# Gated linear attention and retention with their outputs transposed: channels on the partitions, head norm by a product with a 0/1 matrix

## The chip, the cores and the metric

The kernel runs on one core of one Trainium2 chip. A core has five engines with queues of their own: TensorE (PE, matrix products; its weight loads have a row of their own, PEld), VectorE (DVE), ScalarE (ACT), GpSimd (POOL) and SyncE (SP, which here only starts DMA transfers). The metric is the device time of one execution in microseconds (us). The kernel before took 1004.41 us as the median of three runs (1003.13 to 1007.25).

## What is computed

Two layers run over a sequence of 1024 tokens with 1024 features. Each layer normalises and modulates its input, projects it, runs three groups of heads side by side, and projects their concatenation back:

```python
h = rms_norm(x, pre_gain) * (1.0 + scale) + shift
proj = h @ w_in
(aq, ak, av, ag, rq, rk, rv, rg, gq, gk, gv, gg, ga) = jnp.split(proj, IN_SPLITS, axis=-1)
a_out = sliding_window_attention(aq, ak, av, sinks) * jax.nn.silu(ag)
r = retention(rq, rk, rv)                       # 4 heads of 64
r_out = rms_norm(r).reshape(B, S, RET_W) * jax.nn.silu(rg)
log_a = jax.nn.log_sigmoid(ga @ gla_gate_w + gla_gate_b) / 16
g = gated_linear_attention(gq, gk, gv, log_a)   # 4 heads, keys 32 wide, values 64 wide
g_out = rms_norm(g, gla_norm_gain).reshape(B, S, GLA_W) * jax.nn.silu(gg)
y = jnp.concatenate([a_out, r_out, g_out], axis=-1) @ w_out
x = x + gate * rms_norm(y, post_gain)
```

What matters here is the end of the two recurrent groups. Retention and gated linear attention (GLA) each give, per token, four heads of 64 values; every head is divided by the root of its mean square over its 64 values, and the result is multiplied by SiLU of a gate of the same 256 channels.

## The kernel before

The sequence is cut into eight tiles of 128 tokens, and tiles into four pairs. The normalised input of a pair lies transposed in SBUF (`hT`, features on the partitions). A value that needs more than one TensorE pass of precision is split in two parts of type float32r, hi and lo (`split`), and a projection adds three products, hi·hi, lo·hi and hi·lo, over eight slices of 128 features: 24 matrix products (`accum`). Products of plain float32 operands appear in the trace as two records each.

The order of TensorE's instructions is the order in which the program is written out. The program keeps a clock of its own (`clk`), which each product moves on by an assumed cost. Side work stands in jobs (generators), which yield the time that must pass, or the flag that must be set, before their next step. `accum` calls `pump` after every seventh product, and `pump` runs each job that is due. So the latencies in the table `L` (`hn1`, `gz1` and so on) decide between which products of a projection a job's instructions stand; TensorE then waits at run time if the operands are not there. The other engines take their instructions in an order that the framework sets, and SP's queue issues nearly all transfers.

A layer goes through these stages. (1) Gates: for each pair the projections `gg` (GLA's gate, with 16 more columns `ga` for the decay logits: 272 columns) and `rg` (retention's gate), one tile of 128 tokens at a time, tokens on the partitions (`do_gates`, `project`). SiLU of the gate is stored to DRAM (`sgS`, `srS`). `gla_logits` transposes the 16 logit columns and, for every four tiles, `gla_log` turns them into log decays with exp and ln. (2) Retention: per pair the projections `rq`, `rk`, `rv`; a job `ret_core` per tile transposes q and k, forms the scores `sc`, the output `po` and the state `stR`. (3) GLA: projections `gqk` and `gv`, with a job `gla_core` per pair; it uses decays from `gla_decays`, writes masked scores `scz`, the output `po` and the state `stG`. (4) Attention projections, attention, its gate `ag`; (5) the output projection, which reads the concatenated heads from DRAM (`mixS`, and in the second layer `mixF`), with features on the partitions.

Around the change: the output of a tile, `po`, is a PSUM tile with 128 tokens on the partitions and 4 x 64 values on the free axis. In retention (lines 1170 to 1176) the state part is two float32 products of 128 columns, and each head adds one product that holds the head's 128x128 scores as weights and moves 64 columns of values. In GLA (lines 1117 to 1122) the state part is one product of 256 columns, and the heads add the same. PSUM has eight banks, three for projections (`mm`) and five for everything else (`aux`).

`head_norm_gate` (line 960) then squares `po` on ACT (L963), adds up each head on DVE (L965), scales and adds eps (L632), raises to the power -0.5 on POOL (L633), multiplies on DVE (L968), multiplies by the gate loaded from DRAM (L969), waits for `hn1`, transposes the two halves on TensorE (L176), and `store_mix` (L944) splits the transposed tile in hi (ACT) and lo (DVE) and stores both.

The ScalarE keeps one set of function tables at a time; a change of set is an instruction of its own in the trace (ACT_TABLE_LOAD). `gla_log` loads a set with exp and ln each time it runs.

Of the kernel before, what the change touches and what calls it, by code (L numbers as in the profile page):

```python
# [56 lines left out]
def host_constants():  # L57
    f = np.float32
    c = {}
    c["ident"] = np.eye(P, dtype=f)  # L60
    i = np.arange(P)
    rope = np.power(f(10000.0), -np.arange(0, 64, 2, dtype=f) / f(64))
    ret = f(1.0) / np.power(f(10000.0), np.arange(32, dtype=f) / f(31))
    freq = np.concatenate([rope, ret]).astype(f)
    c["freq"] = np.broadcast_to(freq, (P, 64)).copy()
    c["causal"] = (i[:, None] <= i[None, :]).astype(f)
    c["mask2"] = ((i[:, None] <= i[None, :]) & (i[:, None] // 32 == i[None, :] // 32)).astype(np.int32)
    c["curmask"] = (i[:, None] >= i[None, :]).astype(np.int32)
# [12 lines left out]
    c["hmask"] = (i[:, None] // 32 == np.arange(4)[None, :]).astype(f)  # L81
    return c
# [7 lines left out]
def trunk(ctx: ExitStack, tc: tile.TileContext, ins, cst, out):  # L90
# [157 lines left out]
    V.memset(mhalf, -0.5)  # L248

# [4 lines left out]
    sgS = dr.tile([NT, P, 256], F32, name="sgS")  # L254
    srS = dr.tile([NT, P, 256], F32, name="srS")
# [248 lines left out]
    def load(l, name, first=None):  # L504
# [12 lines left out]
        def conv(kc, st):  # L517
# [106 lines left out]
    def project_T(pm, l, hf, w, c):  # L624
# [3 lines left out]
              lambda b, k: both(h0[:, b, k, :], h1[:, b, k, :]))  # L628

# [135 lines left out]
    hmask = cload("hmask")  # L765
    qdec = cload("qdec")
# [177 lines left out]
    def store_mix(l, t, kt0, src, n):  # L944

        if l == DEPTH - 1 and t >= PLAIN:
            mf = t1()
            mfv = mf[:, 0:n * P].rearrange("p (k q) -> p k q", k=n)
            copy("mf", mfv, src)
            dma("smh", mixF[t, :, kt0:kt0 + n, :], mfv)  # L950
# [9 lines left out]
    def head_norm_gate(l, t, po, gate, scale, eps, kt0):  # L960

        sq = t1()
        A.activation(sq, po, AF.Square)  # L963
        ss = small(4)
        V.tensor_reduce(ss, h4(sq), AX.X, ALU.add)  # L965
# [18 lines left out]
    def gla_logits(l, t, pg, pa):  # L984
        ga = small(16)
        A.activation(ga, pa, AF.Copy)
        dma("ssg", sgS[t], silu(pg))
# [10 lines left out]
    def gla_log(l, i):  # L998
# [5 lines left out]
        e, la = t2(), t2()  # L1004
        A.activation(e, z, AF.Abs)
        V.tensor_scalar(la, z, 0.0, None, ALU.min)
        tc.keep_in_program_order(A.preload_act_table_set(TABLES))
# [56 lines left out]
    def gla_core(l, p, qk, vs):  # L1064
# [45 lines left out]
        for c in range(2):  # L1110
# [21 lines left out]
            job(gla_out(l, t, po[:, 0:256]))  # L1132

    def gla_out(l, t, po):
        gate = t1()
        dma("lsg", gate, sgS[t])
        yield from head_norm_gate(l, t, po, gate, 1.0 / 64.0, EPS, 6)
# [8 lines left out]
    def ret_core(l, t, q, k, v):  # L1146
# [24 lines left out]
        for j in range(2):  # L1171
            if t > 0:
# [16 lines left out]
        dma("lsr", sg, srS[t])  # L1189
        yield from head_norm_gate(l, t, po[:, 0:256], sg, 1.0 / 64.0, EPS, 4)  # L1190
# [261 lines left out]
    def layer(l):  # L1452
# [3 lines left out]
        def do_gates(name, p):  # L1456
            w = used(l, name)
            for t in (2 * p, 2 * p + 1):
                pg = mm()
                if name == "gg":  # L1460
                    project(pg[:, 0:272], l, t, w, 272)
                    job(gla_logits(l, t, pg[:, 0:256], pg[:, 256:272]))
                else:
                    project(pg[:, 0:256], l, t, w)
                    dma("ssr", srS[t], silu(pg[:, 0:256]))
# [3 lines left out]
            if name == "gg" and p % 2:  # L1469
                job(gla_log(l, p // 2))  # L1470
# [11 lines left out]
        if l + 1 < DEPTH:  # L1482
            job(mod_all(l + 1, (1, 0), ("mod", l, 2)))
        for p in range(NP_):
# [3 lines left out]
        for p in range(NP_):  # L1488
            last = p == NP_ - 1
            rr = {}  # L1490
            for name in ("rq", "rk", "rv"):
                w = used(l, name)
                for tt in range(2):
                    t = 2 * p + tt
                    pm = mm()
                    project(pm[:, 0:256], l, t, w)
                    src = pm[:, 0:256]
                    if name == "rv":
# [164 lines left out]
L = {"sw1": 0.4, "ld1": 1.2, "ld2": 1.2, "ld1@1": 1.2, "ld2@1": 1.27, "swW00": 0.0, "swT1": 0.0, "swW11": 0.4, "swW10": 0.5, "tt1": 8.0, "tt2": 1.75, "tb1": 24.5, "tb2": 0.75, "pf3": 13.2, "pf1": 6.35, "pf2": 4.16, "mod1": 4.6, "mod2": 4.0, "mod3": 13.29, "mod4": 7.04, "mod5": 3.36, "mod6": 9.04, "pre1": 7.44, "kv1": 3.1, "kv2": 2.11, "aq1": 6.0, "aq7": 6.0, "ag1": 5.44, "aq2": 2.4, "aq6": 5.2, "aq3": 10.21, "aq4": 7.36, "aq5": 3.6, "hn1": 8.93, "hn2": 2.85, "gz1": 11.18, "gz2": 8.13, "gl1": 2.76, "gd3": 15.9, "gc1": 0.62, "gc2": 1.94, "gc3": 1.33, "gc4": 0.87, "gc6": 0.86, "gc5": 1.14, "rc1": 0.8, "rc2": 1.09, "rc3": 5.87, "rc4": 2.51, "fin1": 7.28, "lay1": 1.13, "gc4@1": 0.93, "mod2@1": 4.0, "mod3@1": 15.1, "mod5@1": 3.36, "mod6@1": 4.11, "pre1@1": 7.44, "kv1@1": 2.79, "kv2@1": 5.28, "aq1@1": 4.8, "aq7@1": 5.28, "ag1@1": 6.25, "aq2@1": 0.82, "aq6@1": 6.0, "aq3@1": 10.9, "aq4@1": 4.4, "aq5@1": 5.15, "hn1@1": 8.12, "hn2@1": 2.85, "gz1@1": 15.91, "gz2@1": 10.94, "gl1@1": 4.6, "gd3@1": 15.9, "gc1@1": 0.48, "gc2@1": 1.94, "gc3@1": 1.33, "gc6@1": 0.86, "gc5@1": 1.04, "rc1@1": 0.37, "rc2@1": 0.84, "rc3@1": 1.9, "rc4@1": 2.79, "fin1@1": 4.28, "lay1@1": 1.7}  # L1663
# [35 lines left out]
```

## Time and profile before

| | us |
|---|---|
| median of three runs | 1004.41 |
| the profiled execution, by the same clock as the runs | 1005.52 |
| its span, from the first to the last instruction | 1003.8 |
| TensorE busy | 972.3 |
| VectorE busy | 672.6 |
| ScalarE busy | 411.1 |
| GpSimd busy | 233.8 |

The profiled execution took 1.72 us more than its span, and 1.1 us more than the median. Its mean granted TensorE clock was 0.989 of full speed. Rows of the timeline read: start and length in us from the span's start, engine, source line, operation, output and inputs by the program's names, for a matrix product the rows and columns of its weights and then partitions x columns that are moved, and how many equal records were merged. All products have line 161 and all transposes line 176, since helpers issue them. The length of a matrix product's record holds its latency; records of a run of products overlap, so what a product costs the engine is read from the start of one to the start of the next.

### The profile page before, as it was taken

How to read it: one execution, taken by the hardware profiler on the slowest of the kernel's cores; microseconds unless marked ns; L12 is line 12 of the kernel's file. 1: busy time of each engine (PE TensorE's matmuls, PEld its weight loads, DVE VectorE, ACT ScalarE, POOL GpSimd, SP SyncE). 2: the span in 40 equal slices, each digit the busy share in tenths (PEclk: the TensorE clock that was granted, in tenths of full speed). 3: DMA queues.
4: the chain of work that ended last, by engine and by line, in shares of the span. 5: the costliest groups of instructions: out<-in, count | busy, mean ns of one | idle time of the engine just before them, and what ended most of it. 6: DMA issues, size and time to landing. Idle time of an engine off the chain costs nothing.

```text
span 1003.8 us, 19577 instructions
## 1 busy us (share of the span) xinstructions
PE 972.3 (97%) x7137; PEld 827.1 (82%) x7137; DVE 672.6 (67%) x1645; ACT 411.1 (41%) x1154; POOL 233.8 (23%) x275
## 2 busy tenths in 40 slices
PE   5899999999999999999999999999999999999896
PEld 1599999889998777778889999988899877777675
DVE  3878757768666777664676175775766577567876
ACT  2486312223332666632555332132332257663321
POOL 2310001224320234420122000112322034544100
PEclk8899999999999999999999999999999999999998
DMA  9853413624235355587555241452132434377884
GB/s 316 291 149 98 140 43 100 187 78 115 70 93 178 90 153 168 168 273 235 187 168 169 82 139 34 116 154 84 49 96 85 126 90 135 119 243 241 258 265 142
DMA packets 129836, 148.73 MB, mean 148 GB/s; under 512 B 14046, under 2 KB 94152, under 8 KB 129740
## 3 DMA queue, kind: packets, MB, share of 16 engines
q1 hardware_dynamic: 124044, 137.92, 45.3%
q10 hardware_dynamic: 5696, 9.56, 2.6%
q8 instruction: 56, 0.92, 0.4%
q14 instruction: 40, 0.33, 0.1%
HBM read 109.17 MB, written 36.18 MB: 145 GB/s over the span
## 4 chain that ended last, share of the span: by engine, by line
PE 80%; DVE 8%; DMA 7%; issue 2%; ACT 2%; POOL 1%; SPq 0%; POOLq 0%; DVEq 0%; ACTq 0%
PE mm L161 61%; PE aux L161 14%; PE aux L176 5%; DMA st<-in_w_out_dram 2%; DMA st<-in_w_in_dram 1%; DMA t<-xs 1%; POOL sm L633 1%; DMA t<-aoS 1%; DMA wm<-in_w_mod_dram 1%; DMA xk<-in_x_dram 1%; DVE arena L530 1%; DVE t L1234 1%; DVE t L1331 0%; DVE t L323 0%; DVE st L567 0%
## 5 line engine op out<-in xcount | busy, mean ns | idle before, releaser
L161 PE MATMUL mm<-arena 128*128 128x256 f32 (+2 forms) x1824 | 301.8, 319 | 1.8 <-ACT arena L702 1.8
L161 PE MATMUL mm<-arena,arena 128*128 128x256 f32 (+2 forms) x1824 | 299.0, 317 | 0.0
L161 PEld LDWEIGHTS mm<-arena 128*128 128x128 f32 x1824 | 256.6, 192 | 27.0 <-issue 4.1
L161 PEld LDWEIGHTS mm<-arena,arena 128*128 128x128 f32 x1824 | 252.9, 188 | 25.2 <-issue 4.4
L633 POOL TENSOR_TENSOR sm<-sm,mhalf 128x1 f32<-128x1 f32 (+1 forms) x64 | 56.2, 878 | 348.4 <-DVE sm L632 335.4
L161 PE MATMUL mm<-arena,mx 128*128 128x512 f32 (+1 forms) x564 | 130.9, 388 | 2.2 <-ACT kept L1327 1.9
L161 PEld LDWEIGHTS mm<-arena,mx 128*128 128x128 f32 x564 | 101.6, 188 | 26.6 <-ACT kept L1327 2.3
L145 ACT ACTIVATE t<-aux 128x256 f32<-128x256 f32 (+2 forms) x124 | 55.8, 468 | 76.3 <-PE aux L176 64.8
L145 ACT ACTIVATE arena<-st 128x512 fp32r<-128x512 f32 x94 | 55.6, 626 | 54.6 <-PE mm L161 20.1
L530 POOL TENSOR_TENSOR arena<-st,arena 128x512 fp32r<-128x512 f32 x31 | 43.0, 1389 | 134.4 <-ACT arena L145 97.3
L919 POOL TENSOR_TENSOR smx<-smx,sm 128x512 f32<-128x512 f32 x32 | 36.0, 1126 | 124.2 <-DVE sm L918 110.4
L530 DVE TENSOR_TENSOR arena<-st,arena 128x512 fp32r<-128x512 f32 x77 | 59.6, 795 | 8.0 <-ACT arena L145 5.5
L915 ACT ACTIVATE smx<-smx,sm 128x129 f32<-128x129 f32 x128 | 49.8, 392 | 26.0 <-DVE sm L912 26.0
L360 DVE SCALAR_TENSOR_TENSOR acc<-st,c_act,acc 128x512 f32<-128x512 f32 x60 | 45.4, 757 | 14.9 <-DMA st<-in_w_mod_dram 14.5
L176 PE MATMUL aux<-c_ident,t 128*128 128x128 f32 (+1 forms) x292 | 47.9, 280 | 5.7 <-DVE t L664 5.4
L176 PEld LDWEIGHTS aux<-c_ident,t 128*128 128x128 f32 (+1 forms) x292 | 34.6, 143 | 13.4 <-DVE t L664 7.0
L696 ACT ACTIVATE t<-aux,mod,mod 128x128 f32<-128x128 f32 x68 | 25.9, 459 | 44.0 <-DVE t L1234 18.7
L161 PEld LDWEIGHTS aux<-t,mx 32*128 32x128 f32 (+1 forms) x896 | 39.5, 187 | 3.9 <-issue 2.1
L963 ACT ACTIVATE t<-aux 128x256 f32<-128x256 f32 x32 | 12.3, 383 | 73.8 <-PE aux L161 61.8
L161 PE MATMUL aux<-t,mx 32*128 32x32 f32 (+1 forms) x896 | 40.7, 272 | 0.0
L910 DVE COPY_PREDICATED smx<-c_curmask,aux 128x256 f32<-128x256 int32 x64 | 25.4, 447 | 19.5 <-ACT smx L145 16.0
L1234 DVE SCALAR_TENSOR_TENSOR t<-t,sm,t 128x512 f32<-128x512 f32 x32 | 24.1, 780 | 20.9 <-DMA t<-in_x_dram 11.9
(216 smaller groups left out, 1368.6 us busy)
## 6 DMA issues: line engine op xcount, KB each, us to landing
st<-in_w_in_dram SPq DMA_DIRECT2D x96, 256.0 KB, 3.2
st<-in_w_mod_dram SPq DMA_DIRECT2D x64, 256.0 KB, 3.3
st<-in_w_out_dram SPq DMA_DIRECT2D x52, 256.0 KB, 4.0
mx<-mixS SPq DMA_DIRECT2D x20, 512.0 KB, 7.0
mixS<-t SPq DMA_DIRECT2D x72, 128.0 KB, 2.4
wm<-in_w_mod_dram SPq DMA_DIRECT2D x12, 512.0 KB, 7.1
t<-in_x_dram SPq DMA_DIRECT2D x24, 256.0 KB, 4.6
t<-tabS SPq DMA_DIRECT2D x16, 256.0 KB, 3.5
```

What stands on the lines that cost most here:

```text
L145: A.activation(dst, src, AF.Copy)
L161: T.matmul(dst, lhsT, rhs, start=start, stop=stop)
L176: T.transpose(dst, src, idn)
L360: V.scalar_tensor_tensor(acc, wt, c_act[:, k:k + 1], acc, ALU.mult, ALU.add)
L530: e.tensor_tensor(lo, st, f(hi), ALU.subtract)
L633: G.tensor_tensor(r, r, mhalf[:, :w], ALU.pow)
L696: A.activation(hf[:, ks], at[kt], AF.Identity, scale=gain, bias=shift)
L910: V.copy_predicated(sv, curmask.unsqueeze(1).to_broadcast((P, 2, P)), pv[:, :, n // P - 1, :])
L915: A.activation(sm[:, h, :], sm[:, h, :], AF.Exp, bias=mx[:, h:h + 1], accum_out=sums[:, h:h + 1])
L919: eng("pn").tensor_tensor(sm[:, :, 0:128], sm[:, :, 0:128], rs.unsqueeze(2).to_broadcast((P, 4, P)), ALU.mult)
L963: A.activation(sq, po, AF.Square)
L1234: V.scalar_tensor_tensor(xt[j], yg[j], r, xt[j], ALU.mult, ALU.add)
```

## The change

- The two outputs are formed transposed. For each half j of the 256 channels the state product has the state as weights and moves 128 columns of q; for each head, the 64 columns of its values are the weights, its scores are moved (128 columns), and the product writes 64 partitions of PSUM. `po` has then two heads' channels on the partitions and 128 tokens on the free axis, twice.
- The head norm: ACT squares `po`, a hi and a lo part are made (ACT copy, DVE subtract), and two products with a constant 128x128 matrix `pair` (ones where two channels are of one head) leave each head's sum in all its channels, in the second half of the same PSUM bank. Then ACT takes ln(sum/64 + eps) and exp of -0.5 times that, and DVE multiplies by `po` and by the gate. The sum, scale and power on DVE and POOL and the two transposes are gone, and so is the copy for `mixF`.
- The gates are projected with the weights' columns as output partitions and the 256 tokens of a pair moved at once (`project_P`), so that SiLU(gate) comes out with channels on the partitions. A pair's projection waits for both its tiles. The 16 logit columns go from `gg` (now 256 columns) to `rk` (now 272), so `gla_logits` runs in the retention stage, and `gla_log` is started there by flags.
- `preload_act_table_set` is called once per layer, at the first use of ln.
- The table `L` has new values for most latencies, also outside the changed stages, among them `hn1` 2.4 and 3 (from 8.93 and 8.12 in the two layers), `hn2` 3.5 (2.85), `gz1` 4 and 4.4 (11.18 and 15.91), `rc4` 6.83 and 6.14 (2.51 and 2.79), `ld1@1` 0.59 (1.2).

```diff
+    c["pair"] = (i[:, None] // 64 == i[None, :] // 64).astype(f)
...
             if kc == 3:
-                if name == "gg":
+                if name == "rk":
                     gt = wt[:, :, :, 256:272]
...
+    def project_P(pm, l, p, w, c):
+
+        for t in (2 * p, 2 * p + 1):
+            await_flag(("hT", l, t))
+        h = hT[(l, p)]
+        accum(pm, lambda a, k: w[:, a, k, c:c + P], lambda b, k: h[:, b, k, 0:256])
...
-    def head_norm_gate(l, t, po, gate, scale, eps, kt0):
-
-        sq = t1()
-        A.activation(sq, po, AF.Square)
-        ss = small(4)
-        V.tensor_reduce(ss, h4(sq), AX.X, ALU.add)
-        r = rstd_of(ss, 4, scale, eps)
-        g1 = t1()
-        V.tensor_tensor(h4(g1), h4(po), r.unsqueeze(2).to_broadcast((P, 4, 64)), ALU.mult)
-        eng("hng").tensor_tensor(g1, g1, gate, ALU.mult)
+    def head_norm_gate(l, t, pb, gate, m, kt0):
+
+
+        po, ps_ = pb[:, 0:256], pb[:, 256:512]
+        s, sh, sl = t1(), t1(F32R), t1(F32R)
+        A.activation(s, po, AF.Square)
+        A.activation(sh, s, AF.Copy)
+        V.tensor_tensor(sl, s, f(sh), ALU.subtract)
         yield lat("hn1", l)
-        pt = aux()
-        for j in range(2):
-            transp(pt[:, j * P:(j + 1) * P], g1[:, j * P:(j + 1) * P], ident)
-        store_mix(l, t, kt0, pt[:, 0:256].rearrange("p (k q) -> p k q", k=2), 2)
+        mult(ps_, pair, sh, True, False)
+        mult(ps_, pair, sl, False, True)
+        ln_table(l)
+        A.activation(s, ps_, AF.Ln, scale=m / 64.0, bias=epsc[:, m // 4:m // 4 + 1])
+        A.activation(s, s, AF.Exp, scale=-0.5)
+        V.tensor_tensor(s, po, s, ALU.mult)
+        eng("hng").tensor_tensor(s, s, gate, ALU.mult)
+        store_mix(l, t, kt0, s.rearrange("p (k q) -> p k q", k=2), 2)
...
             po = aux()
-            if t > 0:
-                mult(po[:, 0:256], qb[:, c * P:(c + 1) * P], stG.rearrange("p h d -> p (h d)"), True, False)
-            for h in range(4):
-                mult(po[:, 64 * h:64 * h + 64], scz[:, c, h], v[:, 64 * h:64 * h + 64],
-                     t == 0, t == 0 or h == 3)
+            for j in range(2):
+                cols = slice(j * P, j * P + P)
+                if t > 0:
+                    mult(po[:, cols], stG[:, 2 * j:2 * j + 2, :].rearrange("p h d -> p (h d)"),
+                         qb[:, c * P:(c + 1) * P], True, False)
+                for r in range(2):
+                    h = 2 * j + r
+                    mult(po[64 * r:64 * r + 64, cols], v[:, 64 * h:64 * h + 64], scz[:, c, h], t == 0, True, 0.11)
...
             if t > 0:
-                mult(po[:, j * P:(j + 1) * P], qT[:, j * P:(j + 1) * P], stR[:, j, :], True, False)
-            for h in (2 * j, 2 * j + 1):
-                mult(po[:, 64 * h:64 * h + 64], sc[:, h * P:(h + 1) * P], v[:, 64 * h:64 * h + 64],
-                     t == 0, t == 0 or h % 2 == 1)
+                mult(po[:, cols], stR[:, j, :], qT[:, cols], True, False)
+            for r in range(2):
+                h = 2 * j + r
+                mult(po[64 * r:64 * r + 64, cols], v[:, 64 * h:64 * h + 64], sc[:, h * P:(h + 1) * P], t == 0, True, 0.11)
...
-            for t in (2 * p, 2 * p + 1):
-                pg = mm()
-                if name == "gg":
-                    project(pg[:, 0:272], l, t, w, 272)
-                    job(gla_logits(l, t, pg[:, 0:256], pg[:, 256:272]))
-                else:
-                    project(pg[:, 0:256], l, t, w)
-                    dma("ssr", srS[t], silu(pg[:, 0:256]))
+            d = sgS if name == "gg" else srS
+            for kk in range(2):
+                pg = mm()[:, 0:256]
+                project_P(pg, l, p, w, kk * P)
+                dma("ssg", d[2 * p:2 * p + 2, :, kk].rearrange("t p q -> p t q"), silu(pg).rearrange("p (t q) -> p t q", t=2))
                 pump()
```

More of the change, by code (lines that the diff above doesn't have):

```diff
@@ L248, in trunk, with ln_table @@
     V.memset(mhalf, -0.5)
+    epsc = cp.tile([P, 2], F32, name="epsc")
+    V.memset(epsc[:, 0:1], EPS)
+    V.memset(epsc[:, 1:2], 4.0 * EPS)
+    pin = tc.keep_in_program_order
+    table = [None]
+    def ln_table(l):
+        if table[0] != l:
+            pin(A.preload_act_table_set(TABLES))
+            table[0] = l
     xs = dr.tile([NT, P, D], F32, name="xs")
@@ L253, in trunk @@
     aoS = dr.tile([NT, P, 4, P], F32, name="aoS")
-    sgS = dr.tile([NT, P, 256], F32, name="sgS")
-    srS = dr.tile([NT, P, 256], F32, name="srS")
+    sgS = dr.tile([NT, P, 2, P], F32, name="sgS")
+    srS = dr.tile([NT, P, 2, P], F32, name="srS")
     tabS = dr.tile([NP_, P, 2, 256], F32, name="tabS")
@@ L765, in trunk @@
     hmask = cload("hmask")
+    pair = cp.tile([P, P], F32R, name="pairr")
+    pair_ = t1()[:, 0:P]
+    nc.sync.dma_start(pair_, cst["pair"])
+    A.activation(pair, pair_, AF.Copy)
     qdec = cload("qdec")
@@ L946, in store_mix @@
         if l == DEPTH - 1 and t >= PLAIN:
[L947 to L950, printed above, removed]
+            dma("smh", mixF[t, :, kt0:kt0 + n, :], src)
         mh = t1(F32R)
@@ L1131, in gla_core @@
                 flag(("stG", l, t + 1), lat("gc5", l))
-            job(gla_out(l, t, po[:, 0:256]))
+            job(gla_out(l, t, po))
     def gla_out(l, t, po):
         gate = t1()
-        dma("lsg", gate, sgS[t])
-        yield from head_norm_gate(l, t, po, gate, 1.0 / 64.0, EPS, 6)
+        dma("lsg", gate.rearrange("p (k q) -> p k q", k=2), sgS[t])
+        yield from head_norm_gate(l, t, po, gate, 1, 6)
     def ret_rot(t, src, dec_):
@@ L1188, in ret_core @@
         sg = t1()
-        dma("lsr", sg, srS[t])
-        yield from head_norm_gate(l, t, po[:, 0:256], sg, 1.0 / 64.0, EPS, 4)
+        dma("lsr", sg.rearrange("p (k q) -> p k q", k=2), srS[t])
+        yield from head_norm_gate(l, t, po, sg, 1, 4)
     def y_half(l, t, nh, mixt, ss, yg):
@@ L1483, in layer @@
             job(mod_all(l + 1, (1, 0), ("mod", l, 2)))
+        for i in range(2):
+            job(gla_log(l, i))
         for p in range(NP_):
@@ L1495, in layer @@
                     pm = mm()
-                    project(pm[:, 0:256], l, t, w)
+                    n = 272 if name == "rk" else 256
+                    project(pm[:, 0:n], l, t, w, n)
                     src = pm[:, 0:256]
+                    if name == "rk":
+                        job(gla_logits(l, t, pm[:, 256:272]))
                     if name == "rv":
```

10 lines of the change are left out of this document (4 added, 6 removed).

## Prediction

> **What bounds the kernel now.** I read the page first, then the list of waits, then the groups by form, then the timeline around the outputs of retention and GLA.
>
> ```profile
> span 1003.8 us, 19577 instructions
> PE 972.3 (97%) x7137; PEld 827.1 (82%) x7137; DVE 672.6 (67%) x1645; ACT 411.1 (41%) x1154; POOL 233.8 (23%) x275
> PE 80%; DVE 8%; DMA 7%; issue 2%; ACT 2%; POOL 1%; SPq 0%; POOLq 0%; DVEq 0%; ACTq 0%
> ```
>
> TensorE is busy for 97% of the span and makes 80% of the chain that ended last. The waits say what it still waits for:
>
> ```profile
> PE aux L161 <- ACT t L145: 5.5, 3, 2.3
> PE aux L176 <- DVE t L664: 5.4, 4, 3.1
> PE mm L161 <- ACT kept L1327: 1.9, 1, 1.9
> PE mm L161 <- DVE t L323: 1.2, 1, 1.2
> ```
>
> Between the start and the last output projection only the first row counts: three waits, 5.5 us in all, for a copy on ACT of retention's transposed q and k. So the time is what TensorE's own instructions take, and work taken from POOL, DVE or ACT is worth nothing by itself. The question is what the transposed outputs cost TensorE, and what it newly waits for.
>
> **The outputs, now.** The last tile of retention, and a tile of GLA with its state update behind it:
>
> ```profile
> 204.14 0.39 PE L161 MATMUL mm<-arena,arena 128*128 128x512 f32 x1
> 204.37 0.38 PE L161 MATMUL aux<-stR,t 128*128 128x128 f32 x2
> 204.59 0.56 PE L161 MATMUL aux<-t,t 128*128 128x64 f32 x4
> 204.98 0.44 PE L161 MATMUL aux<-stR,t 128*128 128x128 f32 x2
> 205.26 0.56 PE L161 MATMUL aux<-t,t 128*128 128x64 f32 x4
> 205.63 0.48 PE L161 MATMUL mm<-arena,arena 128*128 128x512 f32 x1
> 231.68 0.59 PE L161 MATMUL aux<-stG,t 128*128 128x256 f32 x2
> 232.11 1.00 PE L161 MATMUL aux<-t,mx 128*128 128x64 f32 x8
> 233.04 0.32 PE L161 MATMUL aux<-t,t 128*32 128x64 f32 x8
> ```
>
> Start to start, retention's output takes 205.63 - 204.37 = 1.26 us: 0.22 for two state records and 0.37 to 0.39 for four head records of 64 columns, so 0.10 each, hardly less than the 0.11 of a record that moves 128. GLA's takes 233.04 - 231.68 = 1.36.
>
> **The outputs, after.** Each head's product then has 64 columns of weights and moves 128. No row has this shape; the nearest is attention's product with the values, weights 128x64, moving 256:
>
> ```profile
> 844.01 0.39 PE L161 MATMUL mm<-arena 128*128 128x512 f32 x1
> 844.33 0.65 PE L161 MATMUL aux<-t,va 128*64 128x256 f32 x4
> 844.91 0.66 PE L176 MATMUL aux<-c_ident,smx 128*128 128x128 f32 x4
> 845.32 0.48 PE L161 MATMUL mm<-arena 128*128 128x512 f32 x1
> 850.65 0.65 PE L161 MATMUL aux<-t,va 128*64 128x256 f32 x4
> 851.13 0.60 PE L161 MATMUL aux<-t,vd 128*64 128x256 f32 x4
> 851.66 0.50 PE L161 MATMUL mm<-arena 128*128 128x512 f32 x1
> 333.94 0.60 PE L176 MATMUL aux<-c_ident,smx 128*128 128x128 f32 x4
> 334.30 0.48 PE L161 MATMUL mm<-arena 128*128 128x512 f32 x1
> ```
>
> Eight such records take 851.66 - 850.65 = 1.01, four take 844.91 - 844.33 = 0.58. The four more cost 0.43, where four full-width records moving 256 columns cost 0.86 (two of GLA's state take 232.11 - 231.68 = 0.43): two heads do run side by side. But 0.58 - 0.43 = 0.15 of every block is something else: the array changes its arrangement. Going in costs more (844.33 - 844.01 = 0.32 after a 512-column record, against 204.37 - 204.14 = 0.23), 0.09; and the four transposes behind it take 845.32 - 844.91 = 0.41 against 334.30 - 333.94 = 0.36, 0.05. So a block of four records carries 0.29 beside its columns. With 128 columns the columns halve to 0.215, and the block is 0.215 + 0.29 = 0.505, where today's takes 0.37 to 0.39.
>
> The Trainium skill's page "TensorEngine Tiling (Array Packing)" speaks for this change under "Performance Considerations": with 64 columns or fewer on the moving side, swap the two operands and use 2x column tiling. The same page speaks against it under "Key Properties": changing the tiling mode drains TensorE. The trace agrees with both: the pairs in the 0.43 for four records, the drain in the 0.29 of a block; the changed order goes from full width to half and back twice in every tile.
>
> Per tile with a state: 2 x (0.22 + 0.505) = 1.45. Retention, 14 such tiles in both layers: (1.45 - 1.26) x 14 = +2.7. GLA: 12 of its 14 are followed by the state update, which uses a narrow arrangement anyway (233.04, 32 columns), so one return of 0.05 falls away: (1.40 - 1.36) x 12 = +0.5; for the other two, whose switch at the end today's 1.36 holds and the last tile has not, I take +0.2 each, +0.4. The four first tiles have no state, and one block of eight records: 0.43 + 0.29 = 0.72 against 0.8 (retention, twice 0.39) to 0.93 (GLA, 233.04 - 232.11) for eight of today's: -0.7 in all.
>
> Bounds: with no cost of changing, a tile is 2 x (0.22 + 0.215) = 0.87, or -5.5 and -6.9 for the two kinds and -1.8 for the first tiles, -14 together. With no pairing either (four records 0.43 and the 0.29) it is 1.88, or +16. I take +2.9, by the row that has the same weights.
>
> **The head norm on TensorE.** Two transposes go, two products of 256 columns come:
>
> ```profile
> 230.73 1.11 PE L161 MATMUL mm<-arena 128*128 128x256 f32 x8
> 211.91 0.38 PE L176 MATMUL aux<-c_ident,t 128*128 128x128 f32 x2
> 212.05 0.60 PE L161 MATMUL mm<-arena 128*128 128x256 f32 x3
> 212.48 0.59 PE L161 MATMUL aux<-acc,c_ones 128*128 128x512 f32 x1
> ```
>
> A 256-column record costs (231.68 - 230.73) / 8 = 0.119. Two transposes with three such behind them take 212.48 - 211.91 = 0.57, so the transposes 0.21; the new pair is 0.24. Over 32 norms +1.0 (bounds 0 and +2).
>
> **The head norm elsewhere.**
>
> ```profile
> 205.85 0.38 ACT L963 ACTIVATE t<-aux 128x256 f32<-128x256 f32 x1 [2.49 <-PE aux L161]
> 206.27 0.42 DVE L965 TENSOR_REDUCE sm<-t 128x4 f32<-128x256 f32 x1 [1.36 <-ACT t L963]
> L633 POOL TENSOR_TENSOR sm<-sm,mhalf 128x4 f32<-128x4 f32 x32 | 35.1, 1098 | 170.1 <-DVE sm L632 167.6 <-DVE gs L1050 1.7 <-PE mm L161 0.6
> 675.11 0.63 ACT L145 ACTIVATE arena<-st 128x512 fp32r<-128x512 f32 x1 [4.76 <-DMA st<-in_w_in_dram]
> ```
>
> POOL loses 35.1 us, DVE swaps one reduction for one subtraction and loses a small scaling; both are hidden behind TensorE and worth 0. ACT gains three operations of 0.38 per norm, 36 us, and loses six table loads and the copies for `mixF`; at 41% busy it has the room. The new wait is TensorE's, at the pair: Square can start 0.22 after the next product has begun (205.85 against 205.63), then 0.38, a copy of 0.38 and a subtraction of 0.42, ready at about 1.4. In the changed program's order 14 to 24 products and more stand between the output and its pair, by the costs above 3.1 to 5.9 us, so the wait is covered with 1.7 to spare. The cover goes where ACT itself stands still in front of the Square: it once waited 4.76 us for a weight transfer. Before, `hn1` held 8.9 us for this. I take +1.0 for all 32 norms, bounds 0 and +5. Behind a waiting pair the rest of the projection is queued, so such a wait counts in full. The longer stay in PSUM costs 0, hidden by four other banks; without them each norm waits for ln, exp and a multiplication, 1.2.
>
> **The gates.** The 24 products of 256 columns per half stay as many, and the 16 logit columns move from `gg` to `rk`: 0. SiLU and the 32 stores stay on ACT and SP, in two pieces of 512 bytes a partition instead of one, plus one transfer of the constant: 0 behind TensorE. The transposes of the logits and `gla_log` come later, with the whole of `rv`'s and `gqk`'s products before the first `gla_core` needs them: 0; without that cover, the chain of a load, abs, exp and ln on ACT, 3 us once a layer. But the first projection of a pair now needs both its tiles:
>
> ```profile
> 68.24 1.03 PE L176 MATMUL aux<-c_ident,t 128*128 128x128 f32 x8
> 69.03 3.19 PE L161 MATMUL mm<-arena,arena 128*128 128x256 f32 x24
> 72.01 0.64 ACT L702 ACTIVATE arena<-t 128x512 fp32r<-128x512 f32 x1
> ```
>
> Tile 5's transposes start at 68.24 and its hi part is complete at 72.65. In the changed order ten products follow them and then the gate of pair 2 begins, at about 70.2, and reaches the second half of the features at 70.7: a wait of up to 1.9; I take +1.4 (bounds 0 and 2.5). Pairs 0, 1 and 3 have half a gate or more in between. At the very start a small split on DVE goes away ahead of the 1.2 us wait for L323, and the first gate waits for a second tile: 0, bounds -1.2 and +0.6.
>
> **Tables and latencies.**
>
> ```profile
> 115.33 1.28 ACT L1007 ACT_TABLE_LOAD   x1
> 117.80 0.71 PE L161 MATMUL aux<-t 64*128 64x128 f32 x8 [0.86 <-ACT t L145]
> ```
>
> One of the three ACT waits comes from a table load and `gla_log` ahead of the copy; both move away: -0.9. The other two waits and the new values of `L` I cannot order from here: 0, bounds -4.6 and +5.5, the waits once more.
>
> **Sum.** 2.9 + 1.0 + 1.0 + 1.4 - 0.9 = +5.4 us. The profiled execution took 1005.5, 1.1 over the median; on the median it is 1004.4 + 5.4, about 1010. A measurement of this kernel can tell about 0.5%, 5 us, from no change.
>
> **Rivals.**
> - *The half-width pairs cost only their columns* (the other side). If going in and out can overlap the full-width products around it, as it cannot in attention, each tile falls to 0.87 and the sum is -14 + 1.0 + 1.0 + 1.4 - 0.9 = -11.5, 993. It pays from where a block's extra is under about 0.22. For it speak the 0.43 for four records; against it that every block I looked at shows the 0.29. The swap rule of the Trainium skill's page "TensorEngine Tiling (Array Packing)", section "Performance Considerations", leads to this.
> - *The change does not move the time.* The extra instructions are there, but the new latencies remove the two remaining ACT waits (-4.6): +0.8, 1005. For it speaks that most of `L` was set anew; against it that these waits come from weight transfers.
> - *TensorE waits at the pairs.* With five more ACT and DVE steps between two parts of a norm, each of 32 norms loses a quarter of a microsecond and the ACT copies come later by as much again as now (+5.5): 1004.4 + 5.4 + 7 + 5.5, some 1022 at most, 1018 as its middle.
>
> **How the numbers follow.** The forecast holds 0.48, with 1006 to 1014 as its own range; 0.5% over the median is 1009.4, so 0.20 of it is no change and 0.28 slower. The pairs at their columns hold 0.13, no change 0.23, the waits 0.16. Faster is 0.13, same 0.43, slower 0.44. The range of 999 to 1018 reaches into the first rival and to the middle of the last.
>
> **What would show it.** Right: in the changed profile two state records, then four head records with 128*64, twice per tile, and 1.4 to 1.5 us from the first to what follows; pairs of 0.24; no ACT_TABLE_LOAD in the retention stage beyond one; a wait of 1 to 2 us at the third pair's gate. Wrong: tiles of 0.9 to 1.1, or waits for ACT or DVE at the pair products that sum to over 3 us. The forecast fails most easily by the 0.29, taken from blocks in attention, and by the new latencies.

## The result and the profile after

The changed kernel took 1014.59 us (median; 1013.64 to 1017.68), the kernel before, with a fourth run, 1004.13 (1003.13 to 1007.25). The ratio is 1.0104, with a 95% interval of 1.0072 to 1.0136: the change costs 10.5 us. The forecast was 1010, with 1006 to 1014 as its own range; the time lies 0.6 above that range and inside the wider one of 999 to 1018. The profiled execution took 1017.68, 3.1 over its median, and 12.2 more than the profiled one of before.

The page of the changed kernel: span, busy times, and the shares of the chain that ended last.

```profile
span 1016.0 us, 19630 instructions
PE 982.6 (97%) x7165; PEld 820.7 (81%) x7165; DVE 673.8 (66%) x1615; ACT 442.2 (44%) x1233; POOL 199.0 (20%) x243
PE 77%; DVE 5%; DMA 4%; ACT 1%; issue 1%; SPq 0%; POOLq 0%; DVEq 0%; ACTq 0%
```

TensorE is still what bounds the kernel; POOL's 35 us are gone, and the kernel is not faster for it. TensorE's waits (who waited, for whom; us in total, times, longest) are others than before:

```profile
PE mm L162 <- ACT arena L721: 5.5, 3, 2.6
PE mm L162 <- ACT arena L549: 2.8, 1, 2.8
PE aux L162 <- ACT t L146: 1.4, 1, 1.4
PE aux L162 <- DVE t L987: 0.3, 1, 0.3
```

Of the three ACT copies that cost 5.5 us before, one is left, with 1.4 (third row). The second row is new: a projection waits 2.8 us for L549, the hi part of the logit columns. In the first row two of the three waits, 2.59 and 0.56, are those of the third pair's gate in layer 0; the third, at 40.8, belongs to the start, where 2.0 us became 2.5. Rows and brackets print the idle time of the engine. Where the text gives a longer figure for the same wait, it is read from the starts of the records: the distance from the start before, less the usual 0.12, which comes out 0.16 longer (2.75 for 2.59, 2.98 for 2.82).

To see where the time went, the same projection product was looked up in both traces by its count, at the borders of the stages (worked out from the starts of the records; small shifts of jobs over a border are in it):

| stage | change against before, us |
|---|---|
| start | -0.1 |
| gates, layer 0 | +1.9 |
| retention, layer 0 | +7.5 |
| GLA, layer 0 | +1.3 |
| attention and output, layer 0 | +0.7 |
| gates, layer 1 | -2.7 |
| retention, layer 1 | +2.4 |
| GLA, layer 1 | +2.0 |
| rest | -1.0 |
| together | +12.0 |

The outputs themselves came out as forecast. The timeline of the changed kernel (start, length, engine, line, operation) has the last tile of retention and a pair of the head norm:

```profile
217.11 0.38 PE L162 MATMUL aux<-t,stR 128*128 128x128 f32 x2
217.42 0.44 PE L162 MATMUL aux<-t,t 128*64 128x128 f32 x4
217.79 0.49 PE L162 MATMUL aux<-t,stR 128*128 128x128 f32 x2
218.21 0.44 PE L162 MATMUL aux<-t,t 128*64 128x128 f32 x4
218.58 1.09 PE L162 MATMUL mm<-arena 128*128 128x256 f32 x7
...
241.91 0.40 PE L162 MATMUL aux<-t,pairr 128*128 128x256 f32 x2
242.15 1.82 PE L162 MATMUL mm<-arena 128*128 128x256 f32 x14
```

The tile takes 218.58 - 217.11 = 1.47 us (forecast 1.45, before 1.26 to 1.28), the pair 0.24. The starts of single records show where the 1.47 goes: the four head records are two pairs of 0.16 and 0.21, against 0.11 for a pair inside a longer block; the second state record takes 0.205 and the first of the next half 0.214, against 0.11. So the array's changes cost about 0.3 us per block, as they did in attention.

The two new waits, first the third pair's (ACT and TensorE), then the one at `rk` (SP's queue, ACT, TensorE):

```profile
67.47 1.03 PE L177 MATMUL aux<-c_ident,t 128*128 128x128 f32 x8
67.75 1.15 ACT L721 ACTIVATE arena<-t 128x512 fp32r<-128x512 f32 x2
68.80 0.63 ACT L668 ACTIVATE t<-t 128x512 f32<-128x512 f32 x1
69.41 0.38 ACT L1002 ACTIVATE t<-mm 128x256 f32<-128x256 f32 x1
69.67 1.51 ACT L715 ACTIVATE t<-aux,mod,mod 128x128 f32<-128x128 f32 x4
71.05 0.66 ACT L146 ACTIVATE arena<-st 128x512 fp32r<-128x512 f32 x1
71.57 0.66 ACT L721 ACTIVATE arena<-t 128x512 fp32r<-128x512 f32 x1
72.28 0.74 PE L162 MATMUL mm<-arena,arena 128*128 128x256 f32 x4 [2.59 <-ACT arena L721]
72.89 0.63 ACT L721 ACTIVATE arena<-t 128x512 fp32r<-128x512 f32 x1 [0.39 <-DVE t L717]
73.57 1.15 PE L162 MATMUL mm<-arena,arena 128*128 128x256 f32 x5 [0.56 <-ACT arena L721]
...
102.78 1.48 SPq L151 DMA_DIRECT2D st<-in_w_mod_dram  x2
104.31 0.43 SPq L548 DMA_DIRECT2D t<-in_w_in_dram  x1
108.21 0.31 ACT L549 ACTIVATE arena<-t 128x128 fp32r<-128x128 f32 x1 [4.70 <-DMA t<-in_w_in_dram]
108.57 1.73 PE L162 MATMUL mm<-arena 128*128 128x272 f32 x6 [2.82 <-ACT arena L549]
```

Tile 5's transposes were over by 68.5, but ACT had the copies of tile 4 (L721 at 67.75), a square (L668) and a SiLU (L1002) to do before it could modulate (69.67), so the hi halves came at 72.23 and 73.52. And the 64 KB of logit columns were asked for at 104.31, behind modulation weights on SP's queue, when `rk`'s other weights were there (in the first experiment below its products start at 103.35); the copy of them began 3.9 us later.

Each wait cost more than itself. The windows around both, of the changed kernel (each line has the window and its length; busy time and records of PE, PEld, DVE, ACT and POOL; the granted clock; the busy share of the DMA engines and GB/s):

```profile
74.00:76.00 2.00, 2.00 (x11) 2.00 (x10) 1.68 (x6) 0.75 (x4) 0.24 (x1) 0.50 0.77 196
76.00:78.00 2.00, 2.00 (x13) 2.00 (x13) 1.85 (x4) 1.32 (x4) 0.31 (x1) 0.66 0.05 12
78.00:82.00 4.00, 4.00 (x37) 4.00 (x36) 3.41 (x8) 1.60 (x4) 0.00 (x0) 1.00 0.35 97
108.00:110.00 2.00, 1.43 (x6) 1.43 (x7) 1.70 (x7) 0.31 (x1) 0.00 (x0) 0.52 0.98 323
110.00:112.00 2.00, 2.00 (x13) 2.00 (x12) 1.74 (x4) 0.00 (x0) 0.00 (x0) 0.63 0.70 210
```

Behind each wait the granted clock stood at half for some 3 us: 11 to 13 records in 2 us where 18 to 20 go at full clock. By the starts, eleven records of 0.227 behind 108.57 instead of 0.125 cost 1.1. Thirty products and transposes from 73.57 on took 5.17, where the same thirty took 3.58 in the trace of the first experiment below, which has no half clock there: 1.6.

### The profile page after: what moved, and what is told of

The parts are those of the page before. It is cut to its first block, busy times and chain, and to the rows that moved or that the text cites. A ratio compares the mean times of both kernels' runs of the same rounds, so it can differ in the third digit from the quotient of the medians.

```text
span 1016.0 us, 19630 instructions
## 1 busy us (share of the span) xinstructions
PE 982.6 (97%) x7165; PEld 820.7 (81%) x7165; DVE 673.8 (66%) x1615; ACT 442.2 (44%) x1233; POOL 199.0 (20%) x243
## 4 chain that ended last, share of the span: by engine, by line
PE 77%; DVE 5%; DMA 4%; ACT 1%; issue 1%; SPq 0%; POOLq 0%; DVEq 0%; ACTq 0%
PE mm L162 58%; PE aux L162 16%; PE aux L177 4%; DMA st<-in_w_in_dram 1%; DMA a<-mixS 1%; DMA st<-in_w_out_dram 1%; DVE arena L542 0%; DMA t<-xs 0%; DMA t<-in_w_in_dram 0%; DMA aoS<-t 0%; DMA t<-aoS 0%; DMA mixF<-t 0%; DVE t L1356 0%; DVE t L1259 0%; ACT t L146 0%
## 5 line engine op out<-in xcount | busy, mean ns | idle before, releaser
L146 ACT ACTIVATE t<-aux 128x512 f32<-128x512 f32 (+1 forms) x80 | 39.7, 507 | 40.7 <-PE aux L177 23.9
L652 POOL TENSOR_TENSOR sm<-sm,mhalf 128x1 f32<-128x1 f32 x32 | 20.1, 630 | 180.2 <-DVE sm L651 165.4
L177 PE MATMUL aux<-c_ident,t 128*128 128x128 f32 (+1 forms) x228 | 36.5, 286 | 5.4 <-DVE t L683 5.4
L715 ACT ACTIVATE t<-aux,mod,mod 128x128 f32<-128x128 f32 x68 | 25.8, 459 | 23.9 <-PE aux L177 12.6
L177 PEld LDWEIGHTS aux<-c_ident,t 128*128 128x128 f32 (+1 forms) x228 | 27.8, 146 | 10.2 <-DVE t L683 6.8
L933 DVE COPY_PREDICATED smx<-c_curmask,aux 128x256 f32<-128x256 int32 x64 | 25.4, 447 | 14.8 <-ACT smx L146 10.5
L985 ACT ACTIVATE t<-aux 128x256 f32<-128x256 f32 x32 | 12.3, 384 | 51.8 <-PE aux L162 45.2
L162 PEld LDWEIGHTS aux<-kT,mx 64*128 64x128 f32 x384 | 24.6, 185 | 11.2 <-issue 8.0
L162 PE MATMUL aux<-kT,mx 64*128 64x256 f32 (+1 forms) x384 | 30.9, 293 | 0.0
```

The source lines that it names most:

```text
L146: A.activation(dst, src, AF.Copy)
L162: T.matmul(dst, lhsT, rhs, start=start, stop=stop)
L177: T.transpose(dst, src, idn)
L652: G.tensor_tensor(r, r, mhalf[:, :w], ALU.pow)
L715: A.activation(hf[:, ks], at[kt], AF.Identity, scale=gain, bias=shift)
L933: V.copy_predicated(sv, curmask.unsqueeze(1).to_broadcast((P, 2, P)), pv[:, :, n // P - 1, :])
```

## The experiments

All are compared with runs of the kernel before on the same chip; medians of before lay between 1005.4 and 1006.9 in them, so ratios are used (the changed kernel: 1.0104). By the widths of the intervals, the difference of two such ratios is known to some 4 us.

**The logit columns early.**

```diff
             dma("lw", st, sv[:, 2 * kc:2 * kc + 2, c0:c0 + 256])
+            if kc == 0 and name == "rk":
+                nc.sync.dma_start(gast, sv[:, :, GA:GA + 16])
             return (st,)
...
-                    nc.sync.dma_start(sg, sv[:, :, GA:GA + 16])
+                    sg = gast
```

> The changed kernel with one transfer moved: the 16 logit columns for rk are requested with rk's first weight piece, into a buffer of their own, instead of after its last. Theory (the wait of 2.98 us ahead of rk's first product at 108.57 is this small transfer, issued at 104.31 behind the modulation's weights on SP's queue): the wait is gone and the time falls by about 3 us, 1011.5. Rival (the products of rk would have waited for something else by then, or the time is given back at the next ACT wait, the 1.6 us at 205.73): less than 1 us, 1014.

1010.69 us, ratio 1.0050 (1.0027 to 1.0072), 0.54% or 5.4 us less than the change. The row for L549 is gone from the waits, and the clock stays up (the same window, of this run):

```profile
108.00:110.00 2.00, 2.00 (x19) 2.00 (x18) 2.00 (x8) 0.15 (x1) 0.00 (x0) 1.00 0.73 242
```

The theory holds. That the gain is larger than its 3 us is within what the ratios leave open, but the trace says so too: retention in layer 0 is 5.6 us shorter, the 2.98 of the wait, 1.1 of slow clock and the 1.6 at 205.73, which did not come back.

**Tile 5 early.**

```diff
-"pf2": 4.28
+"pf2": 2.0
```

> The changed kernel with one latency changed: pf2, the distance between the preparations of tiles 4 to 7, 2.0 instead of 4.28 us, so tile 5's transposes are issued about 2.3 us earlier. Theory (pair 2's first gate waits 2.75 + 0.72 us because tile 5 is late, and nothing but its place in the order makes it late): both waits fall to under 1 us in all and the time falls by 2.5 to 3.5 us, about 1011.5. Rival (ACT, which has the squares, SiLU and weight copies of the same stretch, sets when tile 5 is ready): the waits stay at 2 to 3.5 us and the time at 1013 to 1015.

1018.62 us, 1.0136 (1.0108 to 1.0164): not faster. Neither theory as a whole: the waits of 2.75 and 0.72 at the third pair became 0.92 (at transposes, held by ACT's L715) and 1.34 (at the gate), still in the rival's range, and the gate stage is 2.5 us shorter, but all of it is lost again at `rk`:

```profile
PE mm L162 <- ACT arena L549: 6.3, 1, 6.3
PE mm L162 <- ACT arena L721: 3.6, 2, 2.4
```

Whatever came sooner only stood longer in front of the same transfer.

**One block of head products per tile.**

```diff
             for j in range(2):
                 cols = slice(j * P, j * P + P)
                 if t > 0:
-                    mult(po[:, cols], stG[...], qb[...], True, False)
+                    mult(po[:, cols], stG[...], qb[...], j == 0, False)
+            for j in range(2):
+                cols = slice(j * P, j * P + P)
                 for r in range(2):
...
-                         t == 0, True, 0.11)
+                         t == 0, t == 0 or j == 1, 0.11)
```

(The same in retention.)

> The changed kernel with the products of an output in another order: both state products first, then the four head products in one block, so that TensorE enters and leaves the half-width arrangement once per tile instead of twice. Theory (a change of arrangement costs about 0.3 us for going in and out, beside the columns): a tile with a state falls from 1.47 to about 1.13 to 1.18 us; over 28 tiles 8 to 9.5 us, 1005 to 1006.5. Rival (the 0.3 us belong to the four short products themselves, such as an unhidden load of 64-column weights): the tile stays at 1.4 to 1.5 and the time at 1014.

1009.13 us, 1.0035 (1.0011 to 1.0059), 7 us less than the change. The last tile of retention, as above:

```profile
215.39 0.61 PE L162 MATMUL aux<-t,stR 128*128 128x128 f32 x4
215.93 0.66 PE L162 MATMUL aux<-t,t 128*64 128x128 f32 x8
216.51 1.68 PE L162 MATMUL mm<-arena 128*128 128x256 f32 x12
```

1.12 us. The state records take 0.54 and the head records 0.58, where they took 0.31 + 0.42 and twice 0.37. With the same records and the same weights, one entry and exit fewer saves 0.35 per tile, 9.7 us over all output records (some 2.4 of them went back into waits: 3.46 instead of 2.82 at L549, 1.3 instead of 0.3 at L987, and 0.7 at L1191): the cost belongs to the change of arrangement, not to the short products. The rule of the Trainium skill's page "TensorEngine Tiling (Array Packing)", section "Key Properties", that a change of tiling mode drains TensorE, agrees with it; these rows give 0.3 us as its price here.

**All three.** The three diffs together.

> The changed kernel with the three edits together: logit columns requested early, pf2 at 2.0, one block of head products per tile. Theory (the three costs lie behind one another on TensorE and add): 3 + 3 + 9 = 15 us less, about 1000, faster than the kernel before by some 4 us. Rival (waits that are removed come back at the next transfer or ACT copy): 1005 to 1009.

1001.32 us, 0.9960 (0.9937 to 0.9982): 14 us less than the change and 4 less than before: the theory, within what the ratios can tell. The transfer (5.4) and the blocks (7) add; what pf2 gives is taken up below.

**The parts apart.** Four kernels undo or do one part. "Gates as before" and "outputs alone" share the first diff, "gates alone" is its reverse in the kernel before:

```diff
-            for kk in range(2):
-                pg = mm()[:, 0:256]
-                project_P(pg, l, p, w, kk * P)
-                dma("ssg", d[2 * p:2 * p + 2, :, kk]..., silu(pg)...)
+            for t in (2 * p, 2 * p + 1):
+                pg = mm()
+                n = 272 if name == "gg" else 256
+                project(pg[:, 0:n], l, t, w, n)
+                if name == "gg":
+                    job(gla_logits(l, t, pg[:, 256:272]))
+                dma("ssg", d[t], silu(pg[:, 0:256])...)
...
+            if name == "gg" and p % 2:
+                job(gla_log(l, p // 2))
```

> The changed kernel with the gates as before: projected per tile with the tokens on the partitions, logit columns with gg, gla_log in the gate stage, gz1, gz2 and gl1 of before. Outputs, head norm and the other latencies stay as changed. Left out: the arrangement of the gates, so each head is multiplied by the wrong gates; the work is the same. Theory (the gates cost the two waits of 3.5 and 3.0 us and 1 to 3 us of slow clock behind them; outputs and norm cost TensorE 3 to 4 and 2 to 3 us): no wait at the third pair and at rk, and 4 to 7 us over the kernel before. Rival (the gates are free, the rest is all of it): still 9 to 11 us over the kernel before.

1067.18 us, 1.0603 (1.0565 to 1.0642). The two waits are gone, as the theory says, but waits at other places sum to 32 us after the first 50, and the clock stood at half for 65 us (before: 10 and 3): neither.

> The kernel before with the changed gates alone: projected per pair with channels on the partitions, logit columns with rk, gla_log in the retention stage, the new gz1, gz2 and gl1. Outputs, head norm and the other latencies are those of before. Left out: the arrangement of the gates is not turned back, so each head is multiplied by the wrong gates. Theory: both waits appear here too, 6 to 9 us over the kernel before with the slow clock behind them, less 0.9 for the table load that leaves retention. Rival (moved products cost nothing, the waits belong to the new latencies): within 2 us of the kernel before.

1029.09 us, 1.0237 (1.0209 to 1.0265), 24 over before. Both waits are there without the new outputs: 1.9 and 0.6 us at the third pair, and 6.2 and 5.8 at the logit columns, in both layers here. The rival falls.

```profile
PE mm L161 <- ACT arena L537: 11.6, 2, 6.0
PE aux L161 <- ACT t L145: 5.8, 4, 3.7
```

With the columns asked for early, as in the first experiment:

> The kernel before with the changed gates alone and the logit columns requested with rk's first weight piece. Left out: the arrangement of the gates. Theory (of the 24 us that the gates alone added, 12.0 are the two waits at rk for that small transfer, with 2 to 3 us of slow clock behind them): both waits gone, 7 to 11 us over the kernel before; what is left is the third pair and the logits' new places in ACT's queue. Rival (behind the small transfer the weights of rk are late too): waits of 3 us or more remain at rk, 15 or more over.

1012.38 us, 1.0065 (1.0035 to 1.0094). The first of the two rows is gone: that small transfer was worth 17 us there, 12.0 of waits and the rest of slow clock and what followed. What is left, 6.5 us, lies just under the range expected.

The outputs and the norm alone, with the old gates and all of the old latencies but `hn1` and `hn2`:

> The kernel before with the changed outputs and head norm alone: gates and all latencies as before, only hn1 and hn2 new. Left out: the arrangement of the gates, so each head is multiplied by the wrong gates. Theory (outputs and norm cost TensorE their own records, 3.3 + 0.7 and 2 to 4 us, and few waits where the table fits): 5 to 9 us over the kernel before, with the tiles at 1.47 and the pairs at 0.24. Rival (the longer chain of the head norm, with the old order of everything else, makes TensorE wait): 20 or more over, with waits at the pairs and at the scores of GLA.

1076.87 us, 1.0699 (1.0663 to 1.0736): the rival. Its waits:

```profile
PE aux L162 <- DVE t L994: 16.8, 5, 5.1
PE aux L162 <- ACT t L986: 10.4, 7, 3.0
PE aux L162 <- DVE t L987: 7.2, 4, 2.2
```

The first row is products of GLA that wait for a PSUM bank, which the head norm holds until L994 has multiplied; the other two are the pairs. Neither kernel gives a price of the outputs: the old order of the jobs does not fit the longer norm.

The old latencies in the changed kernel:

```diff
-L = {"sw1": 0.4, "ld1": 1.2, "ld2": 1.33, "ld1@1": 0.59, ...}
+L = {"sw1": 0.4, "ld1": 1.2, "ld2": 1.2, "ld1@1": 1.2, ...}   # but hn1, hn2, gz1, gz2
```

> The changed kernel with the latencies of before, except hn1, hn2, gz1 and gz2, whose jobs are others now. Theory (the new values of the table are worth nothing by themselves): within 3 us of the changed kernel, some 9 to 13 us over the kernel before, with the waits at the third pair and at rk unchanged. Rival (part of the loss is the new values): 3 to 7 us over. Other rival (the new values are what keeps further waits away): 15 or more over.

1051.13 us, 1.0458 (1.0413 to 1.0502), the other rival: 44 over before. The row for L549 is 12.3 in two waits, one of them 6.2 in layer 1, where the changed kernel has none. So in the changed kernel the new table saves time.

**Columns and tile 5 early, two blocks.**

> The changed kernel with the logit columns requested early and pf2 at 2.0, the head products in two blocks as changed. Theory (with pf2 alone the time rose because the wait at rk grew from 3.0 to 6.5 us: the transfer of the logit columns, not TensorE, set when rk could begin; with the columns early the gain at the third pair shows): 2 to 3 us less than with the early columns alone, some 2 to 4 us over the kernel before. Rival (an earlier tile 5 is bad by itself): 6 or more over.

1009.92 us, 1.0045 (1.0023 to 1.0067). 4.5 us over before, close to the 2 to 4 expected, and the loss of pf2 alone is gone with the wait at `rk`; but the gain of 2 to 3 us over the columns alone (1.0050) does not show, so what pf2 is worth stays open.

**One product for the sums of the norm**, in the version with all three edits:

```diff
-        s, sh, sl = t1(), t1(F32R), t1(F32R)
-        A.activation(s, po, AF.Square)
-        A.activation(sh, s, AF.Copy)
-        V.tensor_tensor(sl, s, f(sh), ALU.subtract)
+        s, sh = t1(), t1(F32R)
+        A.activation(sh, po, AF.Square)
         yield lat("hn1", l)
-        mult(ps_, pair, sh, True, False)
-        mult(ps_, pair, sl, False, True)
+        mult(ps_, pair, sh, True, True)
```

> The version with early logit columns, pf2 at 2.0 and one block of head products, and the sums of the head norm in one product: Square writes the hi part at once, and the copy, the subtraction and the second product with the constant are gone. The squares are rounded to float32r, which changes the output slightly. Theory (TensorE is the bound, so each of 32 products counts with its 0.12 us, and the waits of 0.7 and 1.0 us at the pairs go with the shorter chain): 4 to 5.5 us less than with two products, some 8 to 10 us under the kernel before. Rival (another wait ends last at these places): 0 to 2 us less.

1004.60 us, 0.9987 (0.9962 to 1.0012): no gain over two products, the rival. The 32 records are gone, but the program's clock, no longer moved on by them, put jobs elsewhere; new waits came, and 20.5 us of half clock after the start, where the version with two products has none, behind waits of under 1 us (windows of this run):

```profile
748.00:750.00 2.00, 2.00 (x10) 1.94 (x10) 1.97 (x7) 0.65 (x5) 0.00 (x0) 0.50 0.56 163
750.00:752.00 2.00, 2.00 (x11) 2.00 (x11) 2.00 (x8) 1.04 (x2) 0.00 (x0) 0.50 0.91 275
752.00:756.00 4.00, 4.00 (x62) 3.78 (x60) 1.25 (x3) 0.00 (x0) 1.43 (x4) 0.50 0.41 132
```

The last run keeps the order:

```diff
         mult(ps_, pair, sh, True, True)
+        clk[0] += 256 / 2400.0
```

> As the version with one product for the sums of the head norm, but the program's own clock is moved on as if the second product were still there, so every other product of TensorE stands where it stood with two products. The squares are again rounded to float32r. Theory (each removed record is worth its 0.12 us, and what the last run lost came from the moved order, which made waits of 1.6, 1.2 and 0.9 us and stretches of half clock): 3 to 4.5 us less than with two products, 7 to 9 us under the kernel before, clock 0.99 or more. Rival (half clock comes whatever the order): no more than 2 us under the kernel before, clock 0.98.

994.29 us (993.24 to 997.05), 0.9884 (0.9835 to 0.9933): 11.6 under the kernel before and, by the ratios, 22 under the change as it was: the fastest version here. The mean granted clock of its profiled execution was 0.991, against 0.980 in that of the run before it. The gain over two products is 7.6 us by the ratios, known to some 5, so it is not clearly more than the theory's 4.5. The two profiled executions differ by 5.4: 3.8 for 32 records of 0.12 and 1.4 less of listed waits; the two at the pairs (0.45 and 0.87) are gone, and one of 1.08 at 668.61 is new.

## Why the prediction was right, and why only half the size

- *The outputs* (+2.9): right. 1.47 per tile against 1.45, first tiles 0.59 for the eight records and 0.09 more in front of them; all output records together went from 40.5 to 43.8 us, and the state products behind them, which pay the last way out, added 0.9. The rival of pairs at their columns' price, 0.87 per tile, is refuted by the 1.47; with one block per tile it was still 1.12.
- *Pairs for transposes* (+1.0): about -0.5. The 30 pairs of transposes that can be told apart take 0.17, and the product behind them 0.08 more than others, so 0.26 against 0.24.
- *Waits at the pairs* (+1.0): right, 0.40 at 222.13 and 0.44 at 691.22.
- *The third pair's gate* (+1.4, at most 2.5; as a sign of being right, 1 to 2): the mechanism was right, the size was not: 3.5 us in the profiled execution, and 1.6 of slow clock. The forecast took the times from the trace before: TensorE at the gate at 70.2, the hi part complete at 72.65. Here the products ahead of the gate ended 0.7 earlier (the last one starts at 69.41), and the hi part came 0.9 later, at 73.52, since ACT had copies of tile 4, two SiLUs and a weight copy among the steps of tile 5. This execution was the slowest of four; in the two experiments on the logit columns and the blocks, which leave tile 5 alone, the same two waits sum to 2.2 and 2.7.
- *The logit columns from `gg` to `rk`* (0): the step that failed. It counted the columns as products, which they are (in layer 1 retention's grew by 1.0 us and the gates' shrank), and not the transfer that brings them, although the change moves its place on SP's queue to behind modulation weights and directly ahead of its use. 2.98 us of wait and 1.1 to 1.3 of slow clock; moving it gave back 5.4.
- *The table load* (-0.9): right; one load of ln's set per retention stage, at 132.3 and 610.7, and the wait at 117.80 is gone.
- *The other ACT waits and the new latencies* (0, from -4.6): near the lower bound. The wait of 2.43 at 676.28 is gone with its slow clock (at most 1.7, half of a stretch of 3.41), the one of 2.5 is 1.6. And the runs with old latencies show what the zero hid: the same program with the old values is, by the ratios, 36 us slower.
- *Gates, hidden work* (0): the gates' products became a little cheaper (in layer 1 48.0 to 45.9 us, of which 1.0 went to `rk`). The longer stay in PSUM cost nothing in the changed kernel, and 16.8 us where the order did not fit.

So the forecast's 5.4 was right in sign; the two terms at the gates were some 8 us too small with their slow clock, and gains of some 5 us at ACT's waits stood against them: that the total came out within its wider range is in part luck. The sum also priced each wait at its length alone, although the trace before has half clock behind the wait at 676.28 (shown in the last section). The named parts leave about 5 of the 12 us of the profiled execution (which took 3.1 over its kernel's median): 1.5 is half clock at 764 to 767 in GLA, the rest many differences of half a microsecond and less that no run took apart. How much outputs, norm and gates would cost each by themselves in an order that fits them stays open too.

## What to carry to other kernels

Short products that use half of the array pay for entering and leaving that arrangement, 0.3 us here; gather them in one block before judging them by their columns. When an operand's columns move to another product, follow the transfer that brings them, its place on the queue and who stands directly behind it. In a kernel whose order comes from fitted latencies, a part tried alone is measured with the wrong order: keep the order fixed, or fit it again, before calling a step dear or cheap.

## What was unexpected of the hardware

A wait of TensorE cost more than its length. Behind every wait of 2.6 us and more, after the start and in all the traces here, the granted clock went to half, during the wait or up to 2.3 us after its end: after 2.98 us eleven slow records, after 3.6 us (one block) 24 with 2.4 us lost, after 6.5 us (tile 5 early) the first three windows below (of that run). Between 2.0 and 2.5 us it went either way: behind the 2.43 at 676.28 before it fell (fourth window, of the kernel before), behind the 2.50 at 197.17 it stayed at 1.0 (fifth).

```profile
108.00:110.00 2.00, 1.94 (x8) 1.94 (x9) 1.29 (x3) 0.01 (x1) 0.00 (x0) 0.50 0.58 175
110.00:112.00 2.00, 2.00 (x11) 2.00 (x10) 0.00 (x0) 0.00 (x0) 0.00 (x0) 0.50 0.43 127
112.00:114.00 2.00, 2.00 (x15) 2.00 (x14) 0.01 (x1) 0.60 (x1) 0.00 (x0) 0.78 0.05 16
...
678.00:680.00 2.00, 2.00 (x6) 1.61 (x5) 1.59 (x6) 0.00 (x0) 1.62 (x2) 0.50 0.72 216
...
197.00:199.00 2.00, 1.83 (x13) 1.53 (x14) 0.84 (x3) 0.12 (x1) 0.70 (x1) 1.00 0.87 304
```

The records of the granted clock in the traces tell the two apart. Every stretch of half clock up to the last one of a run lasted 3.41 us or two, three or four times that (6.83, 10.24, 13.65), and in each run the borders of all stretches lie whole multiples of 3.413 us apart. Laid on this grid, the wait at 676.28 falls into one interval, with 2.27 us idle, and the one at 197.17 is divided over two, with 1.27 and 1.06. Leaving out the first 50 and the last 30 us, every interval at full clock in which TensorE was idle for 1.8 us or more was followed by half clock. With less it went both ways, and in GLA half clock came at 763.42 in the changed kernel behind an interval of narrow products with 0.1 us idle; what decides there stays open.

The Trainium skill's page "TensorE: Matmul & The Clock Gate" (Part 1: The HAM clock gate) describes such a gate: half clock after an idle window of about 3.4 us, full clock after a busy one, the windows running freely. The rows agree in the two values, and the clock's records in the length of the windows and in borders that do not follow the waits. They differ in what it takes: half clock came behind every such window with 1.8 us of idle time, and in GLA behind one with 0.1, where the page asks for an idle window.
